# A strip copy placed behind a load's wait, and sixteen 64-byte pieces copied first, in a relative-position softmax

## The chip, the cores and the metric

The kernel runs on one core of one Trainium2 chip. Such a core has separate engines that run side by side and meet only at semaphores: VectorE (DVE in the profile), ScalarE (ACT), GpSimd (POOL), SyncE (SP), and TensorE (PE), which this kernel does not use. Data moves between the chip's main memory (DRAM) and the core's on-chip memory by DMA transfers. Here SyncE issues the loads and ScalarE issues the stores; each has a queue of its own, and both queues are worked off by the same 16 DMA engines.

The metric is the device time of one execution in microseconds (us), as a median of several runs. The profile describes one further execution; its span runs from the first to the last instruction of the core.

## The reference, cut to what matters

```python
B, H, S = (2, 8, 2112); max_rel = 16
rel = pos[:, None] - pos[None, :]
rel_clipped = np.clip(rel, -max_rel, max_rel) + max_rel
bias = rel_bias[:, rel_clipped]               # H x S x S
logits = logits + bias[None]
logits = logits - logits.max(axis=-1, keepdims=True)
exp = np.exp(logits)
return exp / exp.sum(axis=-1, keepdims=True)
```

So 2 x 8 x 2112 rows of 2112 float32 numbers are read, each gets a bias that depends only on the head and on the clipped distance between row and column, and each row goes through a softmax and is written. The input and the output have 285.4 MB each.

## The kernel before, in words

**Tiling.** The 33,792 rows are spread over the 128 partitions: partition p owns 264 rows that follow each other in DRAM, so that 8 partitions share one head. The work goes in 44 chunks of R = 6 rows per partition. A chunk is a tile of 128 x 12,672 numbers (6336 KB, or 6.488 MB), and four such tiles, X0 to X3, are used in turn. STEP = 24 rows per partition are one round of the four tiles; there are 11 rounds.

**The bias.** Every row needs the same band of bias values, shifted by one for each row. PSUM, the second on-chip memory, holds one long row of bias values per partition (tile M). `strip(j)` (L179 to L181) copies 2135 of them into the tile F, once in a round of four chunks, and row r of the round reads F at an offset that depends on r.

**A chunk's way.** SyncE loads it (`load`, L79). VectorE adds the bias and finds each row's negated maximum in one instruction per row (`add`, L183 to L190), ScalarE takes exp and the row's sum (`exps`, L192 to L199), and VectorE forms the reciprocals of three rows at a time and scales these rows (`scale`, L201 to L208). ScalarE then issues the store (`store`, L82 to L86). All of this is in place in the tile.

**What sets the order.** Each engine runs its own loop, written out by hand. VectorE's round is the strip, and then for each of the four tiles the wait for its load, six adds, and two halves of scaling. ScalarE's is six exps and a store, for each tile. SyncE's is: wait until the store of a tile has landed, then load the next chunk into that tile. `take` (L74 to L76) waits for a semaphore and lowers it by the same number, so a wait of whichever engine is shown under line 76. There are no costs or due times by which a planner would order anything.

**The start.** VectorE clears F; ScalarE waits for that, and issues a 16.5 KB load of the bias table into F, in 16 pieces (L101 to L107). SyncE issues the load of chunk 0, then a 150 KB load of 15 pieces into part of X3 (L110 to L115), loads 1 and 2, waits for the 15 pieces, and issues load 3 over them. Meanwhile VectorE builds the bias row M from the table (L128 to L177); the first strip follows.

Of the kernel before, what the change touches and what calls it, by code (L numbers as in the profile page):

```python
# [15 lines left out]
def kernel(  # L16
# [6 lines left out]
    nc = tc.nc  # L23
    P = 128
    B, H, S, S2 = logits.shape
# [3 lines left out]
    ROWS = B * H * S // P  # L29
    PB = S // ROWS  # L30
# [8 lines left out]
    FW = S + STEP - 1  # L39
    BIG = 3.0e38  # L40
    LOW, PAD = 32, 2560

    io = ctx.enter_context(tc.tile_pool(name="io", bufs=1))
    X = [io.tile([P, R * S], FP32, tag=f"X{b}", name=f"X{b}") for b in range(NBUF)]
# [9 lines left out]
    def view(t, offset, dims):  # L54

        return bass.AP(tensor=t.tensor, offset=t.offset + offset, ap=[[list(t.ap[0])[0], P]] + dims)

    def rows(t, j, n):

        return bass.AP(tensor=t.tensor, offset=t.offset + j * S, ap=[[ROWS * S, P], [1, n * S]])  # L60

    with tc.tile_critical(no_gpsimd_drain=True):  # L62
        ld = [nc.alloc_semaphore(f"ld{b}") for b in range(NBUF)]
# [6 lines left out]
        idx = nc.alloc_semaphore("idx")  # L70
        dve = nc.alloc_semaphore("dve")
        even = nc.alloc_semaphore("even")
        landed = tc.alloc_semaphore("landed")

        def take(eng, sem, n):
            eng.wait_ge(sem, n).then_inc(sem, -n)  # L76


        def load(j, b):  # L79
            nc.sync.dma_start(out=X[b][:, :], in_=rows(logits, j, R)).then_inc(ld[b], 16)  # L80
# [8 lines left out]
        v = nc.vector  # L89
        done = [0]  # L90

        def then(ins):
            done[0] += 1
            ins.then_inc(dve, 1)

        def settle():
            v.wait_ge(dve, done[0])

        then(v.memset(F[:, 0 : H * W], 0.0))  # L99

        nc.scalar.wait_ge(dve, 1)  # L101
        nc.scalar.dma_start(
            out=bass.AP(tensor=F.tensor, offset=F.offset, ap=[[PB * list(F.ap[0])[0], P // PB], [1, H * W]]),
            in_=bass.AP(
                tensor=rel_bias.tensor, offset=rel_bias.offset, ap=[[0, P // PB], [1, H * W]]
            ),
        ).then_inc(rb, 16)  # L107
        load(0, 0)
        pad = X[NBUF - 1]
        nc.sync.dma_start(  # L110
            out=bass.AP(tensor=pad.tensor, offset=pad.offset + LOW * list(pad.ap[0])[0],
                        ap=[[4 * list(pad.ap[0])[0], 15], [1, PAD]]),
            in_=bass.AP(tensor=logits.tensor, offset=logits.offset + (LOW * ROWS + (NBUF - 1) * R) * S,
                        ap=[[4 * ROWS * S, 15], [1, PAD]]),
# [24 lines left out]
        for m, op in ((eq, ALU.is_equal), (gt, ALU.is_gt), (le, ALU.is_le), (lt, ALU.is_lt)):  # L139
# [4 lines left out]
            out=view(F, 0, [[W, H], [1, W]]), in0=view(F, 0, [[W, H], [1, W]]),  # L144
# [8 lines left out]
                           in_=view(F, RT, [[Q, 2], [PB, Q // PB], [0, PB]])))  # L153
# [9 lines left out]
            out=view(F, 0, [[W, PB], [1, W]]), in0=view(F, SC + 2 * PB, [[1, PB], [0, W]]),  # L163
# [7 lines left out]
            out=view(M, U, [[ROWS, PB], [1, W]]), in0=view(F, 0, [[W, PB], [1, W]]),  # L171
            in1=view(F, SC + 8 * PB, [[1, PB], [0, W]]), op=ALU.add))
        then(v.tensor_copy(out=view(M, U + W, [[ROWS, PB], [1, ROWS - W]]),  # L173
                           in_=view(F, SC + 7 * PB, [[1, PB], [0, ROWS - W]])))
# [4 lines left out]
        def strip(j):  # L179

            v.tensor_copy(out=F[:, :], in_=M[:, bass.ds(ROWS - STEP - j, FW)]).then_inc(dve, 1)  # L181

        def add(b):  # L183
            take(v, ld[b], 16)
            for r in range(b * R, (b + 1) * R):
                x = X[b][:, (r - b * R) * S : (r - b * R + 1) * S]
                v.tensor_tensor_reduce(  # L187
                    out=x, in0=x, in1=F[:, STEP - 1 - r : STEP - 1 - r + S], scale=-1.0, scalar=BIG,
                    op0=ALU.add, op1=ALU.min, accum_out=nmax[:, r : r + 1],
                ).then_inc(added, 1)  # L190
# [10 lines left out]
        def scale(b):  # L201
            for r0 in range(b * R, (b + 1) * R, HALF):
                take(v, expd, HALF)
                v.reciprocal(out=rec[:, r0 : r0 + HALF], in_=tot[:, r0 : r0 + HALF]).then_inc(inv, 1)  # L204
                take(v, inv, 1)
                for r in range(r0, r0 + HALF):
                    x = X[b][:, (r - b * R) * S : (r - b * R + 1) * S]
                    v.tensor_scalar_mul(out=x, in0=x, scalar1=rec[:, r : r + 1]).then_inc(scaled, 1)  # L208

        v.sem_inc(dve, -done[0])  # L210
        with nc.Fori(0, ROWS - STEP + 1, STEP, engines=[ENG.DVE]) as j:  # L211
            strip(j)
            take(v, dve, 1)
            for b in range(NBUF):
                add(b)
                scale(b)
        with nc.Fori(0, ROWS - 2 * STEP + 1, STEP, engines=[ENG.Activation]) as j:
# [48 lines left out]
```

## Time and profile before

| what | us |
|---|---|
| median of 3 runs | 1328.96 (1327.49 to 1329.62) |
| the profiled execution's own time | 1327.58 |
| its span, first to last instruction | 1325.7 |
| VectorE busy in it | 977.9 (74%) |
| ScalarE busy in it | 574.3 (43%) |
| GpSimd busy in it | 0.4 |
| DMA: bytes moved, mean rate | 571.14 MB, 431 GB/s |

The profiled execution took 1.38 us less than the median of the runs, and 1.9 us of its time lie outside its span. An engine's busy time leaves out waiting, branching and the issuing of DMAs; these belong to its sequencer, which the profile marks with a "q" (DVEq, ACTq, SPq). "DMA share" is the mean busy share of the 16 DMA engines. In views of short stretches of time a DMA packet is counted with all its bytes and all its duration in the stretch in which it starts, so the share of a short stretch can exceed 1.

### The profile page before, as it was taken

The numbers are of one execution on the slowest core, as the hardware profiler recorded it, in microseconds if no ns is written. First come the engines' busy times: TensorE is split into PE (matmuls) and PEld (weight loads), VectorE is DVE, ScalarE is ACT, GpSimd is POOL, SyncE is SP. The second block draws the span as 40 slices with busy tenths as digits, with TensorE's granted clock in tenths as the row PEclk, the third lists the DMA queues.
The fourth block names the chain that finished last, engine by engine and source line by source line (L and its number), as shares of the span: only waits on it lengthen the run. The fifth ranks groups of instructions, "written<-read, shape, count | busy, mean of one in ns | idle before, by whom it ended". The sixth has DMA issues, their size and how long they took to land. (4 is left out here: it accounts for less than half of the span.)

```text
span 1325.7 us, 2475 instructions
## 1 busy us (share of the span) xinstructions
DVE 977.9 (74%) x917; ACT 574.3 (43%) x538; POOL 0.4 (0%) x6
## 2 busy tenths in 40 slices
DVE  7998777667877787677778777766877787676774
ACT  3464333434444443334444443433444443333442
POOL 0000000000000000000000000000000000000000
DMA  9999999999999999999999999999999999999998
GB/s 409 419 425 440 437 424 434 440 436 422 437 439 436 425 436 439 428 430 439 440 424 433 440 437 424 436 440 431 428 437 440 425 431 440 439 422 436 439 436 355
DMA packets 12880, 571.14 MB, mean 431 GB/s; under 512 B 1455, under 2 KB 1471, under 8 KB 1471
## 3 DMA queue, kind: packets, MB, share of 16 engines
q1 hardware_dynamic: 6366, 285.63, 49.9%
q10 hardware_dynamic: 6512, 285.49, 49.8%
q14 instruction: 2, 0.02, 0.0%
HBM read 285.65 MB, written 285.47 MB: 431 GB/s over the span
## 5 line engine op out<-in xcount | busy, mean ns | idle before, releaser
L187 DVE CUSTOM_DVE_ANT_0 X<-X,F 128x2112 f32<-128x2112 f32 x264 | 605.2, 2355 | 307.5 <-DVEq L76 307.5
L196 ACT ACTIVATE X<-X,nmax 128x2112 f32<-128x2112 f32 x264 | 541.7, 2052 | 558.4 <-ACTq L76 538.3
L208 DVE TENSOR_SCALAR X<-X,rec 128x2112 f32<-128x2112 f32 x264 | 332.5, 1316 | 13.2
L196 ACT ACT_TABLE_LOAD x10 | 12.8, 1283 | 169.0 <-ACTq L76 169.0
L196 ACT ACTIVATION_READ_ACCUMULATOR X<-X,nmax 128x1 f32 x264 | 49.2, 186 | 0.0
L181 DVE COPY F<-M 128x2135 f32 x11 | 26.1, 2375 | 0.5 <-DVEq L210 0.5
L187 DVE DVE_READ_ACCUMULATOR2_ANT nmax<- 128x1 f32 x264 | 22.0, 83 | 0.0
L204 DVE RECIPROCAL rec<-tot 128x3 f32<-128x3 f32 x88 | 15.0, 171 | 0.0
L143 DVE TENSOR_TENSOR F<-F 128x264 f32<-128x264 f32 x1 | 0.4, 434 | 7.0 <-DMA F<-in_rel_bias_dram 7.0
L173 DVE COPY M<-F 128x1848 f32<-128x1848 f32 x1 | 2.1, 2079 | 0.0
L99 DVE MEMSET F<- 128x264 f32 x1 | 0.3, 278 | 1.1 <-SPq L62 1.1
L147 DVE TENSOR_REDUCE F<-F 128x33 f32<-128x264 f32 x1 | 0.6, 611 | 0.0
L170 DVE TENSOR_TENSOR M<-F 128x264 f32<-128x264 f32 x1 | 0.4, 442 | 0.0
L162 DVE TENSOR_TENSOR F<-F,rbS 128x264 f32<-128x264 f32 x1 | 0.4, 427 | 0.0
L140 DVE TENSOR_SCALAR F<-F 128x8 f32<-128x8 f32 x4 | 0.4, 168 | 0.0
L175 DVE COPY M<-rbS 128x247 f32<-128x247 f32 x1 | 0.4, 408 | 0.0
L150 DVE STREAM_TRANSPOSE F<-F 128x64 f32<-128x64 f32 x1 | 0.2, 245 | 0.0
L155 DVE STREAM_TRANSPOSE F<-F 128x64 f32<-128x64 f32 x1 | 0.2, 245 | 0.0
L160 DVE TENSOR_SCALAR F<-F,rbS 128x8 f32<-128x8 f32 x1 | 0.2, 231 | 0.0
L166 DVE SCALAR_TENSOR_TENSOR F<-F,rbS 128x8 f32<-128x8 f32 x1 | 0.2, 229 | 0.0
L161 DVE TENSOR_SCALAR F<-F,rbS 128x8 f32<-128x8 f32 x1 | 0.2, 225 | 0.0
L167 DVE SCALAR_TENSOR_TENSOR F<-F,rbS 128x8 f32<-128x8 f32 x1 | 0.2, 222 | 0.0
(15 smaller groups left out, 2.1 us busy)
## 6 DMA issues: line engine op xcount, KB each, us to landing
X<-in_logits_dram SPq DMA_DIRECT2D x44, 6336.0 KB, 40.9
out_dram<-X ACTq DMA_DIRECT2D x43, 6336.0 KB, 56.4
out_dram<-X ACTq DMA_DIRECT2D x2, 3168.0 KB, 15.5
X<-in_logits_dram SPq DMA_DIRECT2D x1, 150.0 KB, 17.5
F<-in_rel_bias_dram ACTq DMA_DIRECT2D x1, 16.5 KB, 8.1
```

What stands on the lines that cost most here:

```text
L140: then(v.tensor_scalar(out=m, in0=dp, scalar1=0.0, scalar2=None, op0=op))
L143: then(v.tensor_tensor(out=view(F, 0, [[W, H], [1, W]]), in0=view(F, 0, [[W, H], [1, W]]), in1=view(F, SC + 3 * PB, [[1, H], [0, W]]), op= ...
L147: then(v.tensor_reduce(out=F[:, RB : RB + W], in_=view(F, 0, [[1, W], [W, H]]), axis=mybir.AxisListType.X, op=ALU.add))
L162: then(v.tensor_tensor(out=view(F, 0, [[W, PB], [1, W]]), in0=view(F, SC + 2 * PB, [[1, PB], [0, W]]), in1=view(rbS, W - 1, [[0, PB], [-1, ...
L170: then(v.tensor_tensor(out=view(M, U, [[ROWS, PB], [1, W]]), in0=view(F, 0, [[W, PB], [1, W]]), in1=view(F, SC + 8 * PB, [[1, PB], [0, W]] ...
L173: then(v.tensor_copy(out=view(M, U + W, [[ROWS, PB], [1, ROWS - W]]), in_=view(F, SC + 7 * PB, [[1, PB], [0, ROWS - W]])))
L175: then(v.tensor_copy(out=M[:, 0:U], in_=low.to_broadcast([P, U])))
L181: v.tensor_copy(out=F[:, :], in_=M[:, bass.ds(ROWS - STEP - j, FW)]).then_inc(dve, 1)
L187: v.tensor_tensor_reduce(out=x, in0=x, in1=F[:, STEP - 1 - r : STEP - 1 - r + S], scale=-1.0, scalar=BIG, op0=ALU.add, op1=ALU.min, accum_ ...
L196: nc.scalar.activation(out=x, in_=x, func=EXP, scale=-1.0, bias=nmax[:, r : r + 1], accum_out=tot[:, r : r + 1],).then_inc(expd, 1)
L204: v.reciprocal(out=rec[:, r0 : r0 + HALF], in_=tot[:, r0 : r0 + HALF]).then_inc(inv, 1)
L208: v.tensor_scalar_mul(out=x, in0=x, scalar1=rec[:, r : r + 1]).then_inc(scaled, 1)
```

## The change

Two things are changed.

First, in VectorE's loop the wait for a tile's load moves out of `add` to the head of each turn, and in the turn of tile X0 the strip copy and the wait for its completion come behind that wait. The waits, adds and scalings of the other three tiles stand in the same order as before.

Second, the first instruction of ScalarE is now a DMA that copies 16 pieces of 64 bytes from the logits in DRAM straight to the same places of the output in DRAM: the first 16 numbers of each of the 16 pairs of batch and head. It is issued with no wait before it. Behind the issue of the bias table's load, ScalarE waits until these pieces have landed (`take(nc.scalar, seen, 16)`). Each of the pieces is later overwritten by the store of chunk 0.

```diff
+    MARK = 16
...
+        seen = nc.alloc_semaphore("seen")
...
+        def marks(t):
+
+            return bass.AP(tensor=t.tensor, offset=t.offset, ap=[[PB * ROWS * S, P // PB], [1, MARK]])
+
+        nc.scalar.dma_start(out=marks(out), in_=marks(logits)).then_inc(seen, 16)
         nc.scalar.wait_ge(dve, 1)
         nc.scalar.dma_start(
...
         ).then_inc(rb, 16)
+        take(nc.scalar, seen, 16)
         load(0, 0)
...
         def add(b):
-            take(v, ld[b], 16)
             for r in range(b * R, (b + 1) * R):
...
         with nc.Fori(0, ROWS - STEP + 1, STEP, engines=[ENG.DVE]) as j:
-            strip(j)
-            take(v, dve, 1)
             for b in range(NBUF):
+                take(v, ld[b], 16)
+                if b == 0:
+                    strip(j)
+                    take(v, dve, 1)
                 add(b)
                 scale(b)
```

## The prediction

> **What bounds the kernel now.** I read the page first, then the waits, the DMA issues, short stretches of time, and the order of instructions at four places. The page gives the busy shares, the DMA line and the queues:
>
> ```profile
> span 1325.7 us, 2475 instructions
> DVE 977.9 (74%) x917; ACT 574.3 (43%) x538; POOL 0.4 (0%) x6
> DMA  9999999999999999999999999999999999999998
> DMA packets 12880, 571.14 MB, mean 431 GB/s; under 512 B 1455, under 2 KB 1471, under 8 KB 1471
> q1 hardware_dynamic: 6366, 285.63, 49.9%
> q10 hardware_dynamic: 6512, 285.49, 49.8%
> ```
>
> No engine is busy throughout, but the 16 DMA engines are: SyncE's queue q1 (loads) takes 49.9% of their time and ScalarE's queue q10 (stores) 49.8%. The table of stretches shows how evenly (its last two columns are the DMA share and the rate):
>
> ```profile
> 0.00:10.00 10.00, 1.77 (x13) 0.00 (x0) 0.42 (x6) 1.00 0.83 326
> 10.00:42.00 32.00, 30.33 (x36) 13.62 (x13) 0.00 (x0) 1.00 1.01 436
> 138.00:168.00 30.00, 21.40 (x20) 12.89 (x12) 0.00 (x0) 1.00 1.00 433
> 1248.00:1278.00 30.00, 21.49 (x20) 12.88 (x12) 0.00 (x0) 1.00 1.00 433
> 1320.30:1322.70 2.40, 0.00 (x0) 0.00 (x0) 0.00 (x0) 1.00 0.20 84
> 1322.70:1324.40 1.70, 0.00 (x0) 0.00 (x0) 0.00 (x0) 1.00 0.07 30
> 1324.40:1325.70 1.30, 0.00 (x0) 0.00 (x0) 0.00 (x0) 1.00 0.00 0
> ```
>
> The share is 1.00 early and late in the run. At 433 GB/s the 571.14 MB need 571.14 / 0.433 = 1319.0 us, so of the 1325.7 us only 6.7 are anything but moving bytes at that rate. Two places are visible. The first 10 us run at 326 instead of 433, which is (433 - 326) / 433 x 10 = 2.5 us. After 1320.3 a share of 0.20 is 0.20 x 16 = 3.2 engines, and 0.07 is one: most engines have finished at 1320.3, and a few stragglers work until 1324.4, 4.1 us longer. The bytes are fixed, so a change can win only from these places, and loses only what leaves the DMA engines without work.
>
> The engines' waits say the same from the other side:
>
> ```profile
> ACT X L196 <- ACTq L76: 538.3, 44, 17.2
> DVE X L187 <- DVEq L76: 307.5, 42, 9.0
> ...
> X<-in_logits_dram SPq DMA_DIRECT2D x44, 6336.0 KB, 40.9
> out_dram<-X ACTq DMA_DIRECT2D x43, 6336.0 KB, 56.4
> ...
> F<-in_rel_bias_dram ACTq DMA_DIRECT2D x1, 16.5 KB, 8.1
> ```
>
> VectorE waits 42 times for a load at line 76, 307.5 / 42 = 7.3 us each: it is early everywhere. A chunk's load and store are 2 x 6.488 MB, or 2 x 6.488 / 0.433 = 30.0 us of all engines. A store lands 56.4 us after its issue, so at its issue the store queue still holds about 56.4 - 30.0 = 26 us of older work; the load queue holds 40.9 - 30.0 = 11 us.
>
> **The change: the strip.** One round shows it, from the strip to the next tile's first add:
>
> ```profile
> 107.72 2.37 DVE L181 COPY F<-M 128x2135 f32 x1
> 108.04 0.34 ACTq L84 DMA_DIRECT2D out_dram<-X  x1
> 115.93 2.36 DVE L187 CUSTOM_DVE_ANT_0 X<-X,F 128x2112 f32<-128x2112 f32 x1 [5.84 <-DVEq L76]
> ...
> 137.96 0.34 ACTq L84 DMA_DIRECT2D out_dram<-X  x1
> 146.30 2.36 DVE L187 CUSTOM_DVE_ANT_0 X<-X,F 128x2112 f32<-128x2112 f32 x1 [8.57 <-DVEq L76]
> ```
>
> Before, the copy (2.37 us) runs ahead of a wait that lasts another 5.84 us, so it costs nothing. Afterwards it starts when the load has landed, so the first add comes 2.4 to 2.9 us later: the copy, and up to 0.5 us for its completion wait (bounds 0 and the 0.47 us of idle ahead of the first strip, in the rows below). No instruction is added on VectorE. Behind it wait six adds, six exps, the scalings and the store of that chunk, now issued near 140.6 instead of 137.96. Who notices? The next tile's adds do not: VectorE idles 8.57 us ahead of 146.30 and keeps about 5.9. The store queue does not: it holds some 26 us of older stores and keeps 23. SyncE waits for landings of stores, and these keep their order and pace as long as that queue is not empty. So ten of the eleven strips cost 0. The cover would have to shrink by 23 us before the move of 2.6 us showed, and then it would cost at most 11 x 2.6 = 29 us.
>
> The first strip is different, because only loads are in flight:
>
> ```profile
> 16.02 2.38 DVE L181 COPY F<-M 128x2135 f32 x1 [0.47 <-DVEq L210]
> 19.06 2.36 DVE L187 CUSTOM_DVE_ANT_0 X<-X,F 128x2112 f32<-128x2112 f32 x1 [0.66 <-DVEq L76]
> ...
> 41.11 0.38 ACTq L84 DMA_DIRECT2D out_dram<-X  x1
> ```
>
> Today the copy ends at 18.40 and the load is there 0.66 us later. Afterwards the first add starts near 21.8 and the first store is issued near 43.8. The four loads issued by then are 4 x 6.488 / 0.436 = 59.5 us of work, so the engines stay busy with loads until beyond 60, and the store has some 18 us to spare. Cost 0. The stores as a whole then stand about 2.7 us later against the loads, which only eats into the load queue's 11 us.
>
> At the end the chunk is of tile X3, with no strip ahead of it:
>
> ```profile
> 1285.68 2.36 DVE L187 CUSTOM_DVE_ANT_0 X<-X,F 128x2112 f32<-128x2112 f32 x1 [8.12 <-DVEq L76]
> ...
> 1303.57 4.35 ACTq L84 DMA_DIRECT2D out_dram<-X  x2
> ...
> 1305.00:1320.30 15.30, 2.48 (x3) 0.00 (x0) 0.00 (x0) 1.00 0.98 424
> ```
>
> Its two half stores are issued from 1303.57 on, and the share in the 15.3 us behind 1305 is 0.98: they arrived just about when the older store ran out, with little to spare. A last load that landed some us later would leave all engines dry here. With stores later against loads it should land no later, so I count 0.
>
> **The change: the sixteen pieces.** ScalarE issues one DMA more. The nearest issue is the bias table's, 0.60 us:
>
> ```profile
> 1.40 0.60 ACTq L102 DMA_DIRECT2D F<-in_rel_bias_dram  x1
> ...
> 9.47 0.43 DVE L143 TENSOR_TENSOR F<-F 128x264 f32<-128x264 f32 x1 [7.00 <-DMA F<-in_rel_bias_dram]
> ...
> q1 hardware_dynamic: 16, 0.81, 93.8%
> ...
> q1 hardware_dynamic: 15, 0.76, 141.4%
> ```
>
> The table's load now stands behind that issue and behind the pieces in q10. Its landing ends VectorE's 7.00 us wait; late by between 0 and about 4 us (two turns beside load packets of 1.9 us), it would move the strip of 16.02 to at most 20, hardly past the load that the strip now awaits, and the first store still has over 13 us to spare. The wait on the pieces delays only ScalarE's first exp, which starts past 22. Both cost 0. Of DMA time there are 16 pieces and 16 completion marks, one each per engine, 16 x 64 B = 1 KB; the bound from below is 0, and I take 0.1 us.
>
> The last two rows are q1 in the DMA view of the stretches 40 to 42 and 44 to 46 (packets, MB, share). In the first, 16 load packets take 0.938 x 32 / 16 = 1.88 us each; in the second, 15 take 1.414 x 32 / 15 = 3.02 us. This second stretch is where the first store's packets enter (its issue is the row at 41.11), and every engine loses about 1.1 us once. It may be the price of the first write to the output in DRAM, which the pieces would pay earlier; or of the first switch between the two directions, which they don't spare. No row tells which. The bounds of the gain are 0 and 1.1 us; I take half, -0.5, as the early price would fall into the slow first 10 us only in part.
>
> **Sum:** 0 (strips) + 0.1 (pieces) - 0.5 (first store) = -0.4 us on the profiled execution's 1327.58, which stands 1.38 below the median; on the median of 1328.96 it gives 1328.6.
>
> **Rivals.** *R1, the straggler falls further behind (slower).* The end is that of the slowest engine, now 4.1 us after the bulk. All engines have equal bytes, so its lag comes from slow packets, and the change shifts the phase between loads and stores, on which these may hang. If its lag doubles, the time is 1328.6 + 4.1 = 1332.7. It decides from a lag of 4.1 + 3.0 = 7.1 us on. For it speaks that a lag exists; against it, that three runs agree within 2.1 us.
>
> *R2, the straggler catches up.* If the same shift removes the lag, the time is 1328.6 - 4.1 = 1324.5; with the whole of the first-store loss, 1323.9. It decides from 2.3 us off the lag. For it speaks only that the lag is not in the bytes.
>
> *R3, the pieces hold their engines while they complete (slower).* A DMA of 16.5 KB took 8.1 us to land; if the engines served no load packet during a part of such a time, the whole run would start later by that part. With half of it, 1329.0 + 4.0 = 1333.0. Against it: the rate in the stretch 10 to 42 shows nothing left over from the table's load, and the first 10 us lost only 2.5 us in all. The Trainium skill, page "DMA: Bandwidth & Descriptors", section on the anatomy of one DMA, puts the fixed cost of a transfer at about 2.0 us, most of it the confirmation of the write, heaviest for DRAM. If an engine stood still for that, an estimate by that page is 1329.0 + 2.0 = 1331.0; no run here shows a copy from DRAM to DRAM.
>
> *R4, the first-store loss vanishes whole, nothing else changes:* 1328.6 - 0.6 = 1328.0.
>
> **How the numbers follow.** A measurement of this kernel tells about 0.2%, or 2.7 us, from no change; the bounds are 1326.3 and 1331.6. The forecast has 0.45 and R4 0.18, both within the bounds; R1 has 0.13 and R3 0.05, slower; R2 has 0.19, faster. So faster is 0.19, same 0.63, slower 0.18. The range goes from 1324.8, which takes in most of R2, to 1332.6, close to R1 in full. The forecast's own range is 1327.0 to 1330.5: the sum with either bound of the first-store loss, and 1 us for the spread of the runs.
>
> **What would show it.** The strip should follow line 76's wait directly, near 115.5 in the second round, and the add come some 2.6 us later; the wait of each first tile (5.84 us here) should stand ahead of the strip and be longer by about its 2.4 us; the store issues of each first tile should be later, and the DMA share stay at 1.00 from 10 to 1300. The pieces' effect shows in the q1 packets where the first store enters (1.9 or 3.0 us each), and in the rate of the first 10 us. The forecast is wrong if a stretch in mid run falls clearly below 433 GB/s, if the last load lands later against the stores, or if the few engines behind 1320 become many, or none.

## The result and the profile after

| | median, us | range, us | executions |
|---|---|---|---|
| before | 1328.45 | 1326.88 to 1330.79 | 6 |
| after | 1336.58 | 1330.17 to 1337.13 | 6 |

The ratio after / before is 1.0045 [1.0024, 1.0067]: slower by 0.45%, or 6 us; the medians lie 8.1 us apart, where -0.4 us was forecast, and the new median is outside the range of 1324.8 to 1332.6. Executions of one and the same kernel fall into two groups here, one from 1326 to about 1330 us and one around 1334 to 1338, with a few in between; the change moves executions from the lower group towards the upper one, and the profiled execution of the changed kernel (1330.17 us) is the fastest of its six. That profile thus shows what the change costs at its best. The upper group is shown further down, in the profile of an experiment.

The page of the changed kernel, in the lines that answer to those of before:

```profile
span 1328.3 us, 2477 instructions
DVE 978.6 (74%) x917; ACT 574.5 (43%) x538; POOL 0.4 (0%) x6
...
DMA packets 12912, 571.14 MB, mean 430 GB/s; under 512 B 1487, under 2 KB 1503, under 8 KB 1503
q1 hardware_dynamic: 6366, 285.63, 49.9%
q10 hardware_dynamic: 6544, 285.50, 49.7%
```

The work is the same: 32 small packets more, no instruction more on VectorE, the same bytes. The span is 2.6 us longer. The waits and the DMA issues:

```profile
ACT X L203 <- ACTq L78: 508.0, 34, 19.1
DVE X L194 <- DVEq L78: 219.9, 41, 8.6
DVE F L189 <- DVEq L78: 86.2, 11, 11.3
...
X<-in_logits_dram SPq DMA_DIRECT2D x44, 6336.0 KB, 40.6
out_dram<-X ACTq DMA_DIRECT2D x43, 6336.0 KB, 56.5
...
F<-in_rel_bias_dram ACTq DMA_DIRECT2D x1, 16.5 KB, 11.4
...
out_dram<-in_logits_dram ACTq DMA_DIRECT2D x1, 1.0 KB, 8.3
```

VectorE's waits of 307.5 us have split: 219.9 ahead of adds, and 86.2 ahead of the eleven strips, which now stand behind a load's wait. The table's load takes 11.4 us to land instead of 8.1. Round two, as the timeline has it (start, duration, engine and line; in brackets the idle time ahead):

```profile
120.52 2.38 DVE L189 COPY F<-M 128x2135 f32 x1 [11.28 <-DVEq L78]
...
123.10 2.36 DVE L194 CUSTOM_DVE_ANT_0 X<-X,F 128x2112 f32<-128x2112 f32 x1 [0.20 <-DVEq L78]
...
145.13 0.34 ACTq L86 DMA_DIRECT2D out_dram<-X  x1
...
150.41 2.36 DVE L194 CUSTOM_DVE_ANT_0 X<-X,F 128x2112 f32<-128x2112 f32 x1 [5.52 <-DVEq L78]
```

The strip follows the wait, as forecast, and costs the first add 123.10 - 120.52 = 2.58 us. But this add was at 115.93: it is 7.2 us later, not 2.6, so its load itself landed later, by 120.52 - 115.93 = 4.6 us. The reason is at the start of the kernel:

```profile
0.93 0.66 ACTq L107 DMA_DIRECT2D out_dram<-in_logits_dram  x1
1.62 0.59 ACTq L109 DMA_DIRECT2D F<-in_rel_bias_dram  x1
...
13.10 0.43 DVE L151 TENSOR_TENSOR F<-F 128x264 f32<-128x264 f32 x1 [10.63 <-DMA F<-in_rel_bias_dram]
...
19.77 2.38 DVE L189 COPY F<-M 128x2135 f32 x1 [0.60 <-DVEq L78]
22.35 2.36 DVE L194 CUSTOM_DVE_ANT_0 X<-X,F 128x2112 f32<-128x2112 f32 x1 [0.20 <-DVEq L78]
...
44.39 0.39 ACTq L86 DMA_DIRECT2D out_dram<-X  x1
...
83.83 0.36 SPq L82 DMA_DIRECT2D X<-in_logits_dram  x1
```

The first add comes at 22.35 instead of 19.06, and the first store is issued at 44.39 instead of 41.11, 3.3 us later. The last row is the load of chunk 4, the first that has to wait for a store. Before, the same load stood here:

```profile
76.50 0.36 SPq L80 DMA_DIRECT2D X<-in_logits_dram  x1
```

Loads 0 to 3 wait for no store; the last of them was issued at 19. Load 4 needs tile X0, and so it waits for store 0 to land, which the trace records in 16 parts. Before, all 16 had landed by 76.2. Now eleven land between 77.3 and 78.1, about 2 us later than before, but the other five only between 82.8 and 83.6, and so load 4 is issued 7.3 us later. The DMA view of the stretch 78 to 86 (packets, MB, share of the 16 engines) shows what that does, first before and then after:

```profile
q10 hardware_dynamic: 33, 1.67, 48.3%
q1 hardware_dynamic: 47, 1.57, 45.5%
```

```profile
q10 hardware_dynamic: 64, 2.99, 86.3%
q1 hardware_dynamic: 21, 0.25, 7.7%
```

Before, loads (q1) and stores (q10) shared the engines evenly. After, q1 has 0.25 MB in 8 us, that is 0.25 / 0.0507 = 5 full packets of 50.7 KB. They are the last of load 3, and load 4 has not begun: in the single packets of the trace the next full load packet starts at 87.25, and for the 6.1 us before it the engines move stores alone. They are as busy as before (the two shares add up to 0.94 in both), but loads and stores have shifted against each other, and the shift is paid at the end, where the bytes left over are stores that cannot be issued yet:

```profile
1288.23 2.36 DVE L194 CUSTOM_DVE_ANT_0 X<-X,F 128x2112 f32<-128x2112 f32 x1 [8.11 <-DVEq L78]
...
1306.12 4.35 ACTq L86 DMA_DIRECT2D out_dram<-X  x2
```

```profile
0.00:10.00 10.00, 1.27 (x11) 0.00 (x0) 0.42 (x6) 1.00 0.82 325
...
138.00:168.00 30.00, 24.18 (x23) 14.11 (x14) 0.00 (x0) 1.00 1.00 433
1248.00:1278.00 30.00, 21.55 (x21) 12.89 (x12) 0.00 (x0) 1.00 1.00 433
1305.00:1307.00 2.00, 1.85 (x3) 0.00 (x0) 0.00 (x0) 1.00 0.47 203
1307.00:1322.00 15.00, 3.02 (x3) 0.00 (x0) 0.00 (x0) 1.00 0.98 419
1322.00:1324.80 2.80, 0.00 (x0) 0.00 (x0) 0.00 (x0) 1.00 0.34 145
1324.80:1327.00 2.20, 0.00 (x0) 0.00 (x0) 0.00 (x0) 1.00 0.11 46
```

The chunk of the last load is added at 1288.23 instead of 1285.68, and the last two half stores are issued at 1306.12 instead of 1303.57, both 2.55 us later. The engines run short just ahead of them: a share of 0.47 from 1305 to 1307, where before it was 0.98 from 1305 on. The bulk then ends near 1322 instead of 1320.3, and the stragglers work until 1327.0 instead of 1324.4. In its best execution the change costs 2.6 us, and the median says that it mostly costs 8.

### The profile page after: what moved, and what is told of

It is laid out like the page before. It is cut to its first block, busy times and chain, and to the rows that moved or that the text cites. A ratio compares the mean times of both kernels' runs of the same rounds, so it can differ in the third digit from the quotient of the medians.

```text
span 1328.3 us, 2477 instructions
## 1 busy us (share of the span) xinstructions
DVE 978.6 (74%) x917; ACT 574.5 (43%) x538; POOL 0.4 (0%) x6
## 5 line engine op out<-in xcount | busy, mean ns | idle before, releaser
L194 DVE CUSTOM_DVE_ANT_0 X<-X,F 128x2112 f32<-128x2112 f32 x264 | 605.2, 2354 | 219.9 <-DVEq L78 219.9
L189 DVE COPY F<-M 128x2135 f32 x11 | 26.2, 2381 | 86.2 <-DVEq L78 86.2
L194 DVE DVE_READ_ACCUMULATOR2_ANT nmax<- 128x1 f32 x264 | 21.6, 82 | 0.0
## 6 DMA issues: line engine op xcount, KB each, us to landing
F<-in_rel_bias_dram ACTq DMA_DIRECT2D x1, 16.5 KB, 11.4
```

The source lines that it names most:

```text
L194: v.tensor_tensor_reduce(out=x, in0=x, in1=F[:, STEP - 1 - r : STEP - 1 - r + S], scale=-1.0, scalar=BIG, op0=ALU.add, op1=ALU.min, accum_ ...
```

## The experiments

Beside median and range, each run is read by how many of its executions took more than 1331 us, a line between the two groups. Of the kernel before, 22 of 152 executions did over all comparisons (medians 1327.15 to 1328.45).

### The strip alone, without the pieces

```diff
 def add(b):
-    take(v, ld[b], 16)
...
-    strip(j)
-    take(v, dve, 1)
     for b in range(NBUF):
+        take(v, ld[b], 16)
+        if b == 0:
+            strip(j)
+            take(v, dve, 1)
```

> Only the strip's move, without the sixteen pieces. Theory A (the start's phase: a later first store makes the load of chunk 4 later, the loads stay behind for the whole run, and the DMA engines run dry ahead of the last store): the first add comes near 21.7 instead of 19.06 and the first store near 43.7; the load of chunk 4 is issued some us after 76.5; slower than before by 1 to 6 us. Theory B (the ten later strips cost, each a little): slower by about as much as the whole change, 4 to 8 us. Theory C (the sixteen pieces disturb the DMA engines): as before, within 1.5 us.

Measured: 1336.48 (1327.82 to 1337.73), ratio 1.0042 [1.0021, 1.0064]; 9 of 12 above 1331. The median is 9.1 us above that of the kernel before beside it (1327.38), more than the 1 to 6 of theory A; the times of the start came as it said. The profiled execution belongs to the upper group (1337.23 us, span 1335.4), so it shows what the best execution of the changed kernel could not. Its start, in the timeline:

```profile
21.50 2.36 DVE L186 CUSTOM_DVE_ANT_0 X<-X,F 128x2112 f32<-128x2112 f32 x1 [0.20 <-DVEq L76]
...
43.55 0.38 ACTq L84 DMA_DIRECT2D out_dram<-X  x1
```

These are the times forecast for the strip (21.8 and 43.8). In this execution load 4 is issued at 78.22, and loads do not run out: the DMA view of the stretch 76 to 84 has both queues alike.

```profile
q1 hardware_dynamic: 48, 1.62, 47.0%
q10 hardware_dynamic: 48, 1.62, 47.0%
```

And yet the end looks like this, first in the timeline and then in the table of stretches (last two columns: DMA share and GB/s):

```profile
1293.47 2.36 DVE L186 CUSTOM_DVE_ANT_0 X<-X,F 128x2112 f32<-128x2112 f32 x1 [8.10 <-DVEq L76]
...
1311.36 4.35 ACTq L84 DMA_DIRECT2D out_dram<-X  x2
```

```profile
1308.00:1312.00 4.00, 3.85 (x5) 1.50 (x2) 0.00 (x0) 1.00 0.12 51
...
1314.00:1327.40 13.40, 1.27 (x2) 0.00 (x0) 0.00 (x0) 1.00 0.98 422
1327.40:1334.10 6.70, 0.00 (x0) 0.00 (x0) 0.00 (x0) 1.00 0.06 26
```

The last chunk's add is 1293.47 - 1285.68 = 7.8 us later than before, and so are the last stores. For 4 us a share of 0.12 is 0.12 x 16 = 2 engines: two are behind with older stores, while the others have nothing left. From 1327.4 to 1334.1 a share of 0.06 is one engine, alone for 6.7 us. In mid run (470 to 1270) the DMA view says where such engines fall behind, first the kernel before, then this one:

```profile
q10 hardware_dynamic: 3847, 173.91, 50.2%
q1 hardware_dynamic: 3850, 173.25, 50.0%
```

```profile
q10 hardware_dynamic: 3879, 174.88, 50.5%
q1 hardware_dynamic: 3806, 171.23, 49.7%
```

Full packets have 50,688 bytes (six rows), so before there are 173.25 MB / 50,688 = 3418 load packets, which took 0.500 x 800 x 16 / 3418 = 1.872 us each; here it is 0.497 x 800 x 16 / 3378 = 1.883 us. A store packet took 1.873 us in both. So 3378 load packets took about 0.011 x 3378 = 37 us longer in sum. In the trace's single packets most load packets take 1.87 us as before, and 101 of the 3378 take 0.1 to 1.2 us more, 33 us together. The trace doesn't name a packet's engine, but it has the times of the 16 landings of each store. Those of store 0 lie within 0.7 us; they drift apart in the run, and from near 1110 us on the last comes 22.6 us after the first, and 11.5 us after the last but one. In the kernel before they never lie more than 4.4 us apart. A load is issued only when all 16 parts of a store have landed, so one slow engine holds back the loads of all.

### The pieces alone

```diff
+        nc.scalar.dma_start(out=marks(out), in_=marks(logits)).then_inc(seen, 16)
         nc.scalar.wait_ge(dve, 1)
...
+        take(nc.scalar, seen, 16)
```

> Only the sixteen pieces, with the strip ahead of the wait as before. Theory A: the bias table lands 3.3 us later, so the first add comes near 22.3 as in the changed kernel, and the time is that of the changed kernel, 1330 to 1337. Theory B: as before, within 1.5 us. Theory C: as the changed kernel.

Measured: 1336.73 (1330.65 to 1338.81), 1.0065 [1.0044, 1.0087]; 8 of 9 above 1331. With the strip where it was, the pieces alone are as slow as the whole change. The way is the same: the table lands late, the first add comes at 22.4, the first store at 44.5, load 4 at 84.9. The two parts do not add up; either one delays the start.

### The late strip in the first round only, and in the ten later rounds only

```diff
-        with nc.Fori(0, ROWS - STEP + 1, STEP, engines=[ENG.DVE]) as j:
+        with nc.Fori(0, 1, STEP, engines=[ENG.DVE]) as j:
+            for b in range(NBUF):
+                take(v, ld[b], 16)
+                if b == 0:
+                    strip(j)
+                    take(v, dve, 1)
+                add(b)
+                scale(b)
+        with nc.Fori(STEP, ROWS - STEP + 1, STEP, engines=[ENG.DVE]) as j:
             strip(j)
             take(v, dve, 1)
```

The second kernel has the two loop bodies the other way round.

> No pieces; the strip stands behind the wait in the first round only, and ahead of it in the other ten. Theory A: as the run with the strip's move alone, 1 to 6 us slower than before. Theories B and C: as before, within 1.5 us.

> No pieces; the strip stands ahead of the wait in the first round and behind it in the other ten. Theory A: as before, within 1.5 us, with the load of chunk 4 issued near 76.5. Theory B: as the run with the strip's move alone. Theory C: as before.

Measured, first round only: 1329.26 (1326.70 to 1336.89), 1.0006 [0.9979, 1.0032]; 5 of 12 above 1331. Later rounds only: 1327.69 (1326.73 to 1337.33), 1.0001 [0.9980, 1.0022]; 2 of 12. So ten of the eleven strips cost nothing that the runs can tell, as forecast. The median of the first kernel does not tell it from the one before, but its 5 of 12 stand between 22 of 152 and the 9 of 12 of all strips. Its profiled execution (1336.89 us) ends as the one above does: a share of 0.19 ahead of the last stores, from 1306.0 to 1311.5. Its code starts as that of the strip alone, and yet three of store 0's 16 landings come some 6 us after the others here, and load 4 is issued at 84.52: executions with the same late start differ.

The kernel with the late strip in later rounds shows that slow packets alone are not the cost. In its profiled execution, which took 1328.23 us, the slow load packets between 60 and 1300 us add up to 39 us, against 37 in the slow execution of the strip alone; but the landings of a store never lie more than 3.5 us apart, so no single engine fell behind.

### The pieces behind the table's load

```diff
-        nc.scalar.dma_start(out=marks(out), in_=marks(logits)).then_inc(seen, 16)
         nc.scalar.wait_ge(dve, 1)
...
         ).then_inc(rb, 16)
+        nc.scalar.dma_start(out=marks(out), in_=marks(logits)).then_inc(seen, 16)
         take(nc.scalar, seen, 16)
```

> The changed kernel with the sixteen pieces issued behind the bias table's load instead of ahead of it. Theory A (a later first store thins the load queue, and with a thin load queue most executions lose up to 10 us): the table lands near 9.5 again, the first add comes near 21.6 instead of 22.4, and a part of the executions, as many as with the strip's move alone (about 3 in 4), lies above 1331; median 1330 to 1337. Theory C (the pieces themselves disturb the DMA engines): as the changed kernel, 1336.

Measured: 1329.89 (1327.14 to 1339.05), 1.0026 [1.0001, 1.0052]; 5 of 12 above 1331. The first add is at 21.7, as with the strip alone: the table is no longer late, and about half of the executions return to the lower group. That is a little less slow than theory A expected (3 in 4, median from 1330), and not the 1336 of theory C. What is left is the strip's own move.

### The start later by other means

```diff
+        for _ in range(3):
+            then(v.tensor_copy(out=F[:, :], in_=M[:, 0:FW]))
+            settle()
         v.sem_inc(dve, -done[0])
```

This is the kernel before with three idle copies of VectorE ahead of its loop; strip and waits stand as before.

> The kernel before with three more copies of 2.4 us on VectorE ahead of the first strip, and nothing else. Theory A: the first store is issued near 48.5, the load queue runs dry once for some 7 us, and nearly all executions are slow: median 1335 to 1342. Theory D (how many executions are slow is chance, or belongs to the code of each kernel and not to the start): 1327 to 1329 in four of five executions, as before.

Measured: 1336.54 (1335.45 to 1337.61), 1.0066 [1.0041, 1.0090]; 6 of 6 above 1331. The first add is at 25.97. Neither a piece nor a moved strip is needed to make this kernel slow: a first add that starts 7 us later does it.

### The first store in halves

```diff
+        exps(0)
+        store(0, 0, 0, HALF)
+        store(0, 0, HALF, R - HALF)
...
+            take(nc.sync, st[b], 32 if b == 0 else 16)
...
```

Load 4 waits for both halves; the first rounds of ScalarE and SyncE are written out for it.

> The kernel before with the store of chunk 0 issued in two halves, the first about 4 us earlier. Theory A: the stores start earlier against the loads, the load queue keeps more than its 5 us, and fewer than one execution in five is slow; median 1326 to 1327.5. Theory D: as before, one in five above 1331.

Measured: 1335.58 (1326.36 to 1337.30), 1.0033 [1.0008, 1.0058]; 7 of 12. The expectation failed. The first half store is issued earlier, at 36.8, but load 4 comes later, at 80.2 instead of 76.5: the engines take packets of the two queues in turn, and a half-size store packet (0.94 us) against a whole load packet (1.87 us) gets a third of the time, so the loads ran ahead. The turns agree with the Trainium skill, page "DMA: Bandwidth & Descriptors", section "Queues, rings and completion order", by which an engine goes round its queues packet by packet.

### All transfers in halves

```diff
-            nc.sync.dma_start(out=X[b][:, :], in_=rows(logits, j, R)).then_inc(ld[b], 16)
+            for h in range(0, R, HALF):
+                if wait:
+                    take(nc.sync, su[b] if h else st[b], 16)
+                nc.sync.dma_start(
+                    out=X[b][:, h * S : (h + HALF) * S], in_=rows(logits, j + h, HALF)
+                ).then_inc(ld[b], 16)
```

Stores are split likewise, and each half of a load waits for its own half of the store. This was done to the kernel before and to the changed one.

> The kernel before with every chunk loaded and stored in two halves. If the change costs only by way of slow load packets, which the halves take away: as the changed kernel with halves, 1330 to 1332, and no execution above 1333. If the late start costs something beside them: 1 us or more below the changed kernel with halves, 1326 to 1329.

> The changed kernel with each chunk loaded and stored in two halves of three rows, a half's load waiting only for the landing of its own half's store; the start is as late as in the changed kernel. Theory A: the load queue is refilled some 15 us earlier, never runs dry after the start, and the slow executions are gone: median 1325 to 1329. Theory C or D: as the changed kernel, 1336, or slower because there are twice as many packets.

Measured, on the kernel before: 1329.86 (1329.52 to 1330.97), 1.0013 [0.9996, 1.0030]; none of 11 above 1331. On the changed kernel: 1330.73 (1330.48 to 1332.28), 1.0018 [1.0001, 1.0035]; 3 of 12, and none above 1332.3. The upper group is gone from both, though the second median lies above the 1325 to 1329 of theory A. In the single packets the slow loads are gone too: of some 10,400 load packets in each, one took more than 1.0 us, where 0.94 is usual. There are twice as many packets, as the page of the changed kernel in halves shows:

```profile
DMA packets 25441, 571.16 MB, mean 429 GB/s; under 512 B 2879, under 2 KB 2895, under 8 KB 2895
```

The lowest execution of the kernel before is 1326.0 us, and with halves 1329.5, so halves cost about 3 us. What the change costs without slow packets would be 1330.73 - 1329.86 = 0.9 us; but the two were measured beside different runs of the kernel before (medians 1327.17 and 1327.56), which leaves 0.5 us, and their intervals overlap. So with halves no cost of the late start is shown.

### The loads kept ahead, or held back

Four kernels move loads at the start, to see whether a thin supply of loads makes the packets slow. The first issues the 150 KB load that fills part of X3 behind loads 1 and 2, so that load 3 waits longer; the second adds a small load with a wait of its own ahead of load 3; the third does that to the changed kernel; in the fourth, load 4 waits for a small extra load behind store 0's landing.

The first:

```diff
         load(0, 0)
+        for n in range(1, NBUF - 1):
+            load(n * R, n)
         pad = X[NBUF - 1]
...
-        for n in range(1, NBUF - 1):
-            load(n * R, n)
```

The second and third have beside it, ahead of load 3:

```diff
+        take(nc.sync, even, 16)
+        nc.sync.dma_start(
+            out=bass.AP(tensor=pad.tensor, offset=pad.offset, ap=[[8 * list(pad.ap[0])[0], 16], [1, 64]]),
...
+        ).then_inc(even, 16)
```

The fourth, in SyncE's first round:

```diff
+            take(nc.sync, st[b], 16)
+            if b == 0:
+                nc.sync.dma_start(
...
+                ).then_inc(even, 16)
+                take(nc.sync, even, 16)
+            load(STEP + b * R, b)
```

> The kernel before with the 150 KB load of 15 pieces issued behind loads 1 and 2 instead of ahead of them, so that load 3, which waits for its landing, is issued near 50 instead of 19. From about 48 the engines have the first store alone for some 2 us, so the stores get ahead. Theory A (what counts is how much the load queue still holds when the next load is issued): load 4 is issued near 74, 6 us or more ahead of load 3's landing, and the slow executions become fewer than the one in five of before: median 1326 to 1328. Theory D (the number of slow executions doesn't follow the load queue): one in five or more above 1331.

> As the run before it, with one more small load of 16 pieces of 256 bytes that lands before load 3 is issued, near 54. Theory A: load 4 is issued 8 us or more ahead of load 3's landing; no or hardly any slow execution; median 1326 to 1328. Theory D: one in five or more above 1331.

> The changed kernel with load 3 issued near 54, as in the run before it; the pieces, the late table and the late first store are all kept. Theory A: the load queue is as full as or fuller than in the kernel before, and at most one execution in five is slow; median 1326 to 1329. Theories C (the pieces) and D: as the changed kernel, most executions at 1336.

> The kernel before, with all the compute and the stores at their old times, but load 4 issued only when one more small load of 16 pieces of 256 bytes has landed, which follows load 3 in the load queue: near 86 instead of 76.5, so that the load queue runs dry once for 1 to 4 us. Theory A: half of the executions or more are slow, median 1330 to 1337. A theory by which the late first store itself is what counts, and not the load queue: as before, one in five.

| kernel | median (range) | ratio | above 1331 |
|---|---|---|---|
| first, on before | 1331.73 (1328.68 to 1344.80) | 1.0030 [1.0002, 1.0059] | 7 of 12 |
| second, on before | 1509.87 (1495.68 to 1521.46) | 1.1309 [1.1255, 1.1363] | 6 of 6 |
| third, on after | 1334.12 (1331.85 to 1346.41) | 1.0044 [1.0017, 1.0070] | 12 of 12 |
| fourth, on before | 1337.80 (1330.09 to 1341.69) | 1.0056 [1.0030, 1.0082] | 10 of 12 |

The first three are misses for the theory that a thin supply of loads is the cause. In the first, load 3 is issued at 59.88, some 10 us later than expected (19 in the kernel before), and load 4 within 8 us of it (the row holds both), so that the load queue has over 20 us of work when load 4 is issued,

```profile
59.88 7.99 SPq L80 DMA_DIRECT2D X<-in_logits_dram  x2
```

and still 7 of 12 executions are above 1331. But these kernels try two things at once: while load 3 is held back, there is no load packet at all for 10.5 us from 53.4 on in the first, and for 16.9 and 15.9 us in the second and third, where load 3 is issued at 65.05 and 64.39. A full queue at load 4 is not enough; whether the gap ahead of it spoiled the test is open. The second was the largest surprise; its page and its DMA view from 470 to 1270 have

```profile
DMA packets 12912, 571.15 MB, mean 378 GB/s; under 512 B 1487, under 2 KB 1503, under 8 KB 1503
...
q10 hardware_dynamic: 3380, 152.37, 47.6%
q1 hardware_dynamic: 3362, 151.25, 46.5%
```

the same bytes at 378 GB/s instead of 431. The small load by itself does not do that: the third kernel has it too and took 1334.12. In mid run the packets take about 2.0 us each (152.37 MB / 50,688 = 3006 store packets, 0.476 x 800 x 16 / 3006 = 2.03 us each; loads 1.99) instead of 1.87, and the two shares add up to only 0.94 instead of 1.00, so that about half of the loss is engines without a packet. The fourth came out as expected: the first add and the first store stand at their old times, load 4 is issued at 89.6, and 10 of 12 executions are above 1331. A load 4 that is late is enough.

### The supply without a gap, and a gap in mid run

Only store 0 and load 4 in halves, each half of the load behind its half of the store, on the changed kernel and on the one before; and the kernel before with a small extra load and a wait ahead of the load of chunk 24, in the seventh round.

```diff
+        for h in range(0, R, HALF):
+            take(nc.sync, su if h else st[0], 16)
+            nc.sync.dma_start(
+                out=X[0][:, h * S : (h + HALF) * S], in_=rows(logits, STEP + h, HALF)
+            ).then_inc(ld[0] if h else lh, 16)
```

```diff
+            take(nc.sync, st[b], 16)
+            if b == 0:
+                nc.sync.dma_start(
...
+                ).then_inc(even, 16)
+                take(nc.sync, even, 16)
+            load(6 * STEP + b * R, b)
```

> The changed kernel, with only the store of chunk 0 and the load of chunk 4 cut into two halves of three rows: the first half of load 4 waits only for the first half of store 0. Pieces, late table and late first store are kept. Theory G (a stretch without any load to serve throws the DMA engines out of step, and that makes the slow executions): the first half of load 4 is issued near 70, ahead of load 3's landing near 80, no such stretch is left, and at most one execution in five lies above 1331; median 1326 to 1329. Theory H (it is the late entry of the first store, whatever the loads do after it): as the changed kernel, 5 in 6 above 1331.

> The same halves in the kernel before. Theory G: no stretch without a load, as before or better: at most one in five above 1331, median 1326 to 1328. If half-size packets at the start alone made the slow executions (a reading of the run with the first store in halves): half of the executions above 1331.

> The kernel before, with one more small load in the load queue in the seventh round, for whose landing the load of chunk 24 waits: the load queue is empty once for about 5 us near 685 us, and the start is untouched. Theory G: half of the executions or more are slow, by less than at the start as half of the run is left: 1329 to 1334. Theory H: as before, four in five at 1326 to 1329.

Measured: on the changed kernel 1332.44 (1328.76 to 1337.90), 1.0030 [1.0008, 1.0053], 7 of 12 above 1331; on the one before 1328.98 (1326.46 to 1337.16), 1.0014 [0.9990, 1.0039], 4 of 12. In the changed kernel the first half of load 4 is now issued 13 us earlier, and no stretch without a load packet is longer than 3.0 us:

```profile
70.68 15.51 SPq L260 DMA_DIRECT2D X<-in_logits_dram  x2
```

7 of 12 is fewer than 17 of 18 of the changed kernel and its run again (below), and far more than the one in five that a gap as the only cause would leave. So the gap may be one part and is not the whole. The 4 of 12 on the kernel before cannot be told from its own 22 of 152.

With the gap in mid run (9.8 us without a load packet, from 684.3 on): 1331.11 (1328.72 to 1416.06), 1.0019 [0.9997, 1.0041]. One execution of 1416.06 stands far apart from all others and is left out of the ratio; of the other eleven, 5 are above 1331. Even its lowest execution is 2.7 us above the lowest of the kernel before, 1326.0. A gap in the loads was paid for at both places that were tried, at load 4 and in mid run.

### The change once more, and the change with the start restored

> The changed kernel once more, for more executions and a second profile: 5 in 6 above 1331, most at 1336 to 1338; in a profile of such an execution one to three DMA engines end several us after the others, with more than 10 us of slow load packets (all theories).

Measured: 1336.00 (1331.74 to 1338.64), 1.0052 [1.0033, 1.0070]; 12 of 12 above 1331. The result stands. The profile fell on the lowest execution (1331.74), so it does not show the upper group, for which it was taken.

The last kernel keeps all of the change but for its late start: the pieces go behind the table's load, and only the first strip is put ahead of its wait again. Ten late strips and sixteen pieces are left.

```diff
-        with nc.Fori(0, ROWS - STEP + 1, STEP, engines=[ENG.DVE]) as j:
+        with nc.Fori(0, 1, STEP, engines=[ENG.DVE]) as j:
+            strip(j)
+            take(v, dve, 1)
+            for b in range(NBUF):
+                take(v, ld[b], 16)
+                add(b)
+                scale(b)
+        with nc.Fori(STEP, ROWS - STEP + 1, STEP, engines=[ENG.DVE]) as j:
```

> The changed kernel with the sixteen pieces issued behind the bias table's load and the first strip ahead of the first wait; the pieces and the ten later late strips are kept. If the start is all that counts: first add near 19, first store near 41, at most one or two executions in ten above 1331, median 1326.5 to 1328.5. If the pieces or the later strips have a part: a third or more above 1331.

Measured: 1327.34 (1326.06 to 1336.79), 1.0000 [0.9982, 1.0017]; 1 of 12 above 1331. In its timeline the first add and load 4 are back at their old times (19.06 and 76.50):

```profile
18.93 2.36 DVE L194 CUSTOM_DVE_ANT_0 X<-X,F 128x2112 f32<-128x2112 f32 x1 [0.83 <-DVEq L78]
...
76.82 0.36 SPq L82 DMA_DIRECT2D X<-in_logits_dram  x1
```

With the start at its old time nothing of the cost is left that these runs can tell. The late start is thus what makes the change slow. The runs without halves or moved loads, ordered by their first add:

| kernels | first add, us | load 4 issued, us | above 1331 |
|---|---|---|---|
| before; late strips in later rounds; start restored | 18.9 to 19.1 | 76 to 77 | 25 of 176 |
| strip alone; first round only; pieces behind the table | 21.5 to 21.8 | 78 to 85 | 19 of 36 |
| the change; the change again; pieces alone | 22.3 to 22.6 | 84 to 85 | 25 of 27 |
| three idle copies | 26.0 | 79.8 | 6 of 6 |

No kernel was faster than the one before.

The profiled executions can also be ordered by how far the engines drifted apart. Left out are the kernels with all transfers in halves, and the three that hold load 3 back, in which the landings of loads lie 14 to 50 us apart too. The third column is the longest stretch up to 110 us in which no full load packet was under way, the last the longest time between the first and the last of a store's 16 landings, both from the single records of the trace:

| profiled executions | time, us | without loads, us | landings apart, us |
|---|---|---|---|
| before; late strips in later rounds; start restored | 1327.4 to 1328.2 | 1.0 to 1.4 | 3.5 to 5.3 |
| gap in mid run | 1329.9 | 1.4 | 5.6 |
| load 4 held back | 1330.1 | 10.2 | 4.3 |
| the change; again; pieces alone; pieces behind the table; first store in halves | 1330.0 to 1331.7 | 6.1 to 8.3 | 9.0 to 12.9 |
| store 0 and load 4 in halves, on after | 1332.6 | 3.0 | 14.7 |
| the same, on before | 1336.6 | 0.9 | 18.7 |
| strip alone; first round only; three idle copies | 1335.5 to 1337.2 | 3.0 to 8.7 | 20.1 to 22.7 |

With a gap in the loads and little drift an execution took some 2.5 us more (second and third row, both among the faster ones of their runs); those of the upper group here are the ones whose landings have drifted 18 us and more apart, with a gap or without.

## Why the prediction was wrong, step by step

- **What bounds the kernel: right.** The DMA engines, before and after, with 433 GB/s in mid run.
- **Ten later strips cost 0: right** (2 of 12 above 1331 with these alone; 1 of 12 with the pieces beside them). The strip's 2.4 to 2.9 us was 2.58.
- **The first strip costs 0: this step failed.** The strip alone moved the first add to 21.50 and the first store to 43.55, as worked out (21.8 and 43.8). The failure is in what was asked of these times. The step asked whether the engines stay busy until the store enters, and they do. What hangs on the store's landing was not followed: load 4 waits for all 16 parts of it, and loads 0 to 3 wait for no store, so the loads stop where the store is not through. In the changed kernel load 4 is 7.3 us later for a store issued 3.3 us later: most of the store's 16 parts landed 2 us later than before, and five another 5 us after the others.
- **"Only eats into the load queue's 11 us": this failed too.** The 11 us came from a median landing time over 44 loads. At load 4 the queue had 9.3 us: load 4 was issued at 76.5, and load 3 had landed at 85.8. After the change load 3 has landed at 83.4, load 4 is issued at 83.83, and nothing is left.
- **The last load "should land no later": failed.** Four tiles close a loop: a load waits for a store, a store for its load. Late stores therefore mean late loads. The chunk of the last load is added 2.55 us later in the best execution and 7.8 us later in the upper group that the strip alone showed; the engines run dry ahead of the last stores, at the place that the prediction pointed out as having little to spare. This was one of the things named as making the forecast wrong.
- **The table late by 0 to 4 us: right in size (3.3 us), wrong in price.** The strip moved to 19.77, as bounded (20 at most), hardly later than by its own move alone (18.93 with the strip alone), and this was counted as nothing because the first store was thought to have over 13 us to spare. The pieces alone, with only this delay, put 8 of 9 executions above 1331.
- **First-store loss, -0.5: wrong.** The first store entered in the stretch 46 to 48, in the DMA view of the changed kernel:

```profile
q1 hardware_dynamic: 16, 0.81, 145.4%
```

That is 1.454 x 32 / 16 = 2.91 us per load packet, against 3.02 before. An earlier write to the output spares 0.1 us at most, not half of 1.1, and even that is within the scatter: with late strips in later rounds, without any pieces, these load packets took 2.79 us. R4 falls with it.
- **The pieces' DMA time, 0.1 us, and R3:** the first 10 us moved 325 GB/s against 326, and the pieces landed in 8.3 us. The engines did not stand still for them. The estimate of 2.0 us lost is not borne out by the trace. The Trainium skill, page "DMA: Bandwidth & Descriptors", section on the anatomy of one DMA, gives that cost for transfers issued by GpSimd; these were issued by ScalarE.
- **R1, a straggler that falls further behind: this is what happened**, in the upper group, and it had a chance of 0.13. Its price was put at 4.1 us from a doubled lag of one engine's end; 8 to 9 were measured, because an engine that is behind does not only end late, it holds back the loads of all 16 engines, and these run dry ahead of the last stores. In the slow profiles of the strip alone, the first round only and the idle copies the landings of a store come to lie 20 to 23 us apart, where 4.4 was the most before. Three executions within 2.1 us were held against R1; over 152, the kernel before shows the same group 22 times. R2 did not occur.

**What stays open** is why a later start lets single engines fall behind. Slow load packets go with it in the strip alone, but not everywhere: as many cost nothing with late strips in later rounds, and with the pieces alone the landings of the second store already lie 12 us apart, while no load packet from 470 to 1270 us is slow. Taken alone, none of these explains it: a gap in the loads (7 of 12 above 1331 without one over 3.0 us, and none longer in the slow profile of the strip alone), a thin supply of loads (7 of 12 with a full one at load 4, though behind a gap), the pieces, or the later strips. A late load 4 alone suffices (10 of 12), and transfers of half the size take the upper group away. That points to how whole loads and stores stand to each other in time, which no run here resolved further; the second kernel of the moved loads, at 1509.87 us, may be the same thing on all engines, or not.

## What to carry to other kernels

Where transfers are the bound and a few buffers close a loop (a load waits for a store, the store for its load), follow a delay at the start round the whole loop: the first load that must wait tells whether the delay has cover, not a median landing time. A wait far from the bottleneck can be free ten times and cost everything the first time, so a change in a loop is to be costed for its first turn separately. And where executions fall into two groups, three times are too few to hold against the slower one; a change can move the share without moving either group, as the strip alone did.

## What was not expected of the hardware

- A start later by 3 us shows mostly in the share of executions: 25 of 176 above 1331 with the first add at 19, 19 of 36 with it at 21.6, 25 of 27 with it at 22.4. At 21.6 the lowest executions are still at 1326.7 to 1327.8; at 22.4 they are shifted too, to 1330.2 at the lowest.
- Single load packets of 50,688 bytes took 0.1 to 1.2 us longer than the usual 1.87 in the slow profile of the strip alone, and one of the 16 parts of a store landed up to 22.6 us after the first; with packets of 25,344 bytes the slow packets were gone, at a price of about 3 us for twice the packets.
- Load 3 held back by a small load with a wait cost 13% on the kernel before (1509.87 us, 378 GB/s), by packets of 2.0 us instead of 1.87 and engines without a packet for 6% of the time; the same edit on the changed kernel gave 1334.12.
- A 1 KB copy on the same queue ahead of a 16.5 KB load delayed its landing from 8.1 to 11.4 us, beside full load packets.
